# A small store on every DMA engine, and gamma in four pieces, at the start of an RMSNorm + SiLU kernel

**The chip, the cores, the metric.** One core of one Trainium2 chip. The metric is device time of one execution in microseconds (us); less is better. "Span" is what the profile covers, from the first to the last instruction; time was about 1.8 us more than the span (319.27 against 317.5 in the execution profiled before the change).

## The reference

```python
def reference(x, gamma, eps):          # x: 8 x 1024 x 2048 float32, gamma: 2048
    rms = np.sqrt(np.mean(x ** 2, axis=-1, keepdims=True) + eps)
    out = gamma * x / rms
    return (out * (1 / (1 + np.exp(-out)))).astype(np.float32)
```

Each of the 8192 rows is read once and written once: 67.11 MB in and 67.11 MB out.

## The kernel before

The rows are cut into 16 blocks of 4 MB: 128 partitions with 4 rows, 32 KB, each. Six buffers go round. SP issues the loads, ACT the stores. A load into a buffer waits until the store of the block before it in that buffer has landed (store 0 landed at 64.32 us, and load 6 was issued at 64.38). Gamma is put into all 128 partitions (`g`): it is loaded into one partition, spread by matmuls with a column of ones into PSUM, and copied.

```python
    def load(b):
        xt = pool.tile([P, J * d], f32, name="xt")     # P=128, J=4, d=2048; 6 buffers
        nc.sync.dma_start(out=xt, in_=xb[b])
        blocks[b] = xt
    ...
    def store(b):
        nc.scalar.dma_start(out=ob[b], in_=blocks[b])
        if b + LEAD < nblk:                            # LEAD = 6
            load(b + LEAD)
    ...
        grow = pool.tile([P, J * d], f32, name="xt")
        nc.scalar.dma_start(out=grow[0:1, 0:d], in_=<gamma as one row>)
        for b in range(min(LEAD, BUFS - 1)):           # loads 0 to 4
            load(b)
        nc.vector.memset(ones, 1.0)
        for c in range(0, d, 512):
            nc.tensor.matmul(junk_v[:, c:c + 512], ones, grow[0:1, c:c + 512], start=True, stop=True)
        nc.vector.tensor_copy(out=g, in_=junk_v)
        load(BUFS - 1)
        last = nblk - 1
        sums(0)          # sums of squares: row 3 on DVE, rows 0 to 2 on ACT
        ...
```

Of the kernel before, what the change touches and what calls it, by code (L numbers as in the profile page):

```python
# [1 line left out]

# [4 lines left out]

ACT = mybir.ActivationFunctionType
ALU = mybir.AluOpType


@with_exitstack
def kernel(
    ctx: ExitStack,
    tc: tile.TileContext,
    x: bass.AP,
    gamma: bass.AP,
    eps: bass.AP,
    out: bass.AP,
):  # L20





    nc = tc.nc
    P = nc.NUM_PARTITIONS
    f32, i32 = mybir.dt.float32, mybir.dt.int32
    x2 = x.flatten_outer_dims()
    o2 = out.flatten_outer_dims()  # L30
    n, d = x2.shape
    J = 4
    BUFS, LEAD = 6, 6
    nblk = n // (P * J)
    xb = x2.rearrange("(b p j) d -> b p (j d)", p=P, j=J)
    ob = o2.rearrange("(b p j) d -> b p (j d)", p=P, j=J)

    singles = ctx.enter_context(tc.tile_pool(name="singles", bufs=1))
    pool = ctx.enter_context(tc.tile_pool(name="pool", bufs=BUFS))
    small = ctx.enter_context(tc.tile_pool(name="small", bufs=2))  # L40
    psum = ctx.enter_context(tc.tile_pool(name="psum", bufs=1, space=bass.MemoryType.PSUM))

    g = singles.tile([P, d], f32)
    ones = singles.tile([1, P], f32)
    junk_a = psum.tile([P, d], f32, name="junk_a")
    junk_v = psum.tile([P, d], f32, name="junk_v")
    blocks, sss, rstds = {}, {}, {}

    def load(b):
        xt = pool.tile([P, J * d], f32, name="xt")  # L50
        nc.sync.dma_start(out=xt, in_=xb[b])
        blocks[b] = xt

    def row(b, j):
        return blocks[b][:, j * d:(j + 1) * d]

    def rsqrt(ss):


        var = small.tile([P, J], f32, name="var")  # L60
        nc.vector.tensor_scalar(out=var, in0=ss, scalar1=1.0 / d, scalar2=float(eps),  # L61
                                op0=ALU.mult, op1=ALU.add)
        y = small.tile([P, J], f32, name="y")
        t = small.tile([P, J], f32, name="t")
        nc.vector.tensor_single_scalar(out=t.bitcast(i32), in_=var.bitcast(i32), scalar=1,  # L65
                                       op=ALU.logical_shift_right)
        nc.vector.tensor_scalar(out=y.bitcast(i32), in0=t.bitcast(i32), scalar1=-1, scalar2=0x5F375A00,  # L67
                                op0=ALU.mult, op1=ALU.add)
        for _ in range(3):
            nc.vector.scalar_tensor_tensor(out=t, in0=y, scalar=-0.5, in1=y, op0=ALU.mult, op1=ALU.mult)  # L70
            nc.vector.tensor_mul(out=t, in0=t, in1=var)  # L71
            nc.vector.scalar_tensor_tensor(out=y, in0=t, scalar=1.5, in1=y, op0=ALU.add, op1=ALU.mult)  # L72
        return y

    def sums(b, after_first=()):


        ss = small.tile([P, J], f32, name="ss")
        nc.vector.tensor_tensor_reduce(  # L79
            out=junk_v, in0=row(b, J - 1), in1=row(b, J - 1), scale=1.0, scalar=0.0,  # L80
            op0=ALU.mult, op1=ALU.add, accum_out=ss[:, J - 1:J])
        for j in range(J - 1):
            nc.scalar.activation(out=junk_a, in_=row(b, j), func=ACT.Square,  # L83
                                 accum_out=ss[:, j:j + 1])
            if j == 0:
                for s in after_first:
                    store(s)
        sss[b] = ss

    def finish(b, pieces=1):  # L90
        for j in range(J):
            nc.vector.tensor_mul(out=row(b, j), in0=row(b, j), in1=g)  # L92
            nc.scalar.activation(out=row(b, j), in_=row(b, j), func=ACT.Silu,  # L93
                                 scale=rstds[b][:, j:j + 1])
            if pieces > 1 and (j + 1) % (J // pieces) == 0:
                w = J // pieces * d
                i = (j + 1) // (J // pieces) - 1
                nc.scalar.dma_start(out=ob[b][:, i * w:(i + 1) * w], in_=blocks[b][:, i * w:(i + 1) * w])  # L98

    def store(b):  # L100
        nc.scalar.dma_start(out=ob[b], in_=blocks[b])  # L101
        if b + LEAD < nblk:
            load(b + LEAD)

    with tc.manual_schedule():
        grow = pool.tile([P, J * d], f32, name="xt")
        nc.scalar.dma_start(out=grow[0:1, 0:d],
                            in_=bass.AP(tensor=gamma.tensor, offset=gamma.offset, ap=[[d, 1], gamma.ap[0]]))
        for b in range(min(LEAD, BUFS - 1)):
            load(b)  # L110
        nc.vector.memset(ones, 1.0)  # L111
        for c in range(0, d, 512):
            nc.tensor.matmul(junk_v[:, c:c + 512], ones, grow[0:1, c:c + 512], start=True, stop=True)  # L113
        nc.vector.tensor_copy(out=g, in_=junk_v)  # L114
        load(BUFS - 1)


        last = nblk - 1
        sums(0)
        rstds[0] = rsqrt(sss[0])  # L120
        finish(0)
        sums(1)
        rstds[1] = rsqrt(sss[1])
        for b in range(1, last - 1):
            sums(b + 1, after_first=[b - 1])
            finish(b)
            rstds[b + 1] = rsqrt(sss[b + 1])
        store(last - 2)
        finish(last - 1)
        store(last - 1)  # L130
        sums(last)
        rstds[last] = rsqrt(sss[last])
        finish(last, pieces=2)


# [1 line left out]
_INS = ['x', 'gamma', 'eps']  # L137
_OUTS = [((8, 1024, 2048), 'float32')]

_NUMBERS = {'eps': 9.999999747378752e-06}  # L140


# [26 lines left out]
```

## Time and profile before

| | |
|---|---|
| time, 3 runs known at the prediction | 317.92 us median (317.8 to 318.91) |
| time of the execution that was profiled | 319.27 us |
| span of that execution | 317.5 us |
| data through the 16 DMA engines | 134.26 MB, mean 423 GB/s |
| busiest compute engine | ACT, 70% |

The rows of the profile are shown in the prediction below. The DMA row in tenths is full from the second slice to the last but one, and the two data queues hold 98.4% of the engines' span, so the kernel is bound by the DMA engines. The page does not print single packets; the trace has a record of each (queue, start, duration, size), and much of what follows is read from these. A 32 KB packet on an undisturbed engine takes 1.213 us (96% of them in the profile before).

### The profile page before, as it was taken

What the parts mean: (1) busy time and instruction counts of PE and PEld (TensorE: products, weight loads), DVE (VectorE), ACT (ScalarE), POOL (GpSimd) and SP (SyncE); (2) the same over time, 40 slices, a digit from 0 to 9 for tenths busy, and PEclk for the clock granted to TensorE, in tenths of its full rate; (3) what the DMA queues carried; (4) which work ended last, traced back from release to release, by engine and by line L of the source; (5) the groups of instructions that cost most, each with busy time, mean ns of one, the idle gap of its engine ahead of it and who ended that gap; (6) DMA issues with size and microseconds to landing.
All of it is one profiled execution on the core that took longest, in us unless ns stands there. A gap on an engine that the chain in (4) does not pass through costs nothing.

```text
span 317.5 us, 603 instructions
## 1 busy us (share of the span) xinstructions
PE 7.2 (2%) x8; PEld 2.5 (1%) x8; DVE 210.3 (66%) x290; ACT 221.3 (70%) x162; POOL 0.2 (0%) x4
## 2 busy tenths in 40 slices
PE   6200000000000000000000000000000000000000
PEld 2000000000000000000000000000000000000000
DVE  0559299999892947839287392974929559946600
ACT  1359989999892947939388393984929659794800
POOL 0000000000000000000000000000000000000000
DMA  8999999999999999999999999999999999999994
GB/s 327 429 433 433 425 392 455 405 454 417 442 430 433 425 438 425 433 446 425 438 425 439 417 442 433 425 458 417 442 417 446 413 446 433 430 446 425 438 411 204
DMA packets 4758, 134.26 MB, mean 423 GB/s; under 512 B 529, under 2 KB 529, under 8 KB 529
## 3 DMA queue, kind: packets, MB, share of 16 engines
q1 hardware_dynamic: 2304, 67.11, 49.4%
q10 hardware_dynamic: 2450, 67.12, 49.0%
q14 instruction: 4, 0.03, 0.0%
HBM read 67.12 MB, written 67.11 MB: 423 GB/s over the span
## 4 chain that ended last, share of the span: by engine, by line
DMA 73%; DVE 11%; ACT 7%; issue 3%; DVEq 1%; ACTq 0%; SPq 0%
DMA xt<-in_x_dram 39%; DMA out_dram<-xt 34%; DVE xt L92 8%; ACT junk_a L83 5%; ACT xt L93 3%; DVE junk_v L79 1%; DVEq L164 1%; DVE t L70 0%; DVE t L71 0%; DVE y L72 0%; DVE t L65 0%; DVE y L67 0%; DVE var L61 0%; ACTq L98 0%; ACTq L101 0%
## 5 line engine op out<-in xcount | busy, mean ns | idle before, releaser
L92 DVE TENSOR_TENSOR xt<-xt,g 128x2048 f32<-128x2048 f32 x64 | 142.3, 2285 | 0.0
L83 ACT ACTIVATE junk_a<-xt 128x2048 f32<-128x2048 f32 x48 | 90.3, 1881 | 65.5 <-DMA xt<-in_x_dram 64.0
L93 ACT ACTIVATE xt<-xt,y 128x2048 f32<-128x2048 f32 x64 | 124.0, 1992 | 13.0 <-DVE xt L92 13.0
L79 DVE CUSTOM_DVE_ANT_0 junk_v<-xt 128x2048 f32<-128x2048 f32 x16 | 36.8, 2299 | 57.5 <-DMA xt<-in_x_dram 57.5
L61 DVE TENSOR_SCALAR var<-ss 128x4 f32<-128x4 f32 x16 | 2.6, 166 | 15.7 <-ACT junk_a L83 15.7
L83 ACT ACTIVATION_READ_ACCUMULATOR junk_a<-xt 128x1 f32 x48 | 9.0, 187 | 0.0
L72 DVE SCALAR_TENSOR_TENSOR y<-t,y 128x4 f32<-128x4 f32 x48 | 7.8, 162 | 1.7
L70 DVE SCALAR_TENSOR_TENSOR t<-y 128x4 f32<-128x4 f32 x48 | 7.8, 162 | 1.7
L71 DVE TENSOR_TENSOR t<-t,var 128x4 f32<-128x4 f32 x48 | 7.8, 162 | 1.6
L114 DVE COPY g<-junk_v 128x2048 f32<-128x2048 f32 x1 | 2.3, 2292 | 8.7 <-PE junk_v L113 8.7
L113 PE MATMUL junk_v<-xt,ones 1*128 1x512 f32 x8 | 7.2, 1072 | 2.5 <-DMA xt<-in_gamma_dram 2.5
L67 DVE TENSOR_SCALAR y<-t 128x4 int32<-128x4 int32 x16 | 2.7, 170 | 0.5
L65 DVE TENSOR_SCALAR t<-var 128x4 int32<-128x4 int32 x16 | 2.7, 170 | 0.5
L113 PEld LDWEIGHTS junk_v<-xt,ones 1*128 1x128 f32 x8 | 2.5, 325 | 5.6 <-issue 5.6
L79 DVE DVE_READ_ACCUMULATOR2_ANT ss<- 128x1 f32 x16 | 2.3, 142 | 0.0
L83 ACT ACT_TABLE_LOAD x1 | 1.3, 1283 | 1.3 <-PEq L150 1.3
L93 ACT ACT_TABLE_LOAD x1 | 1.3, 1283 | 0.0
L111 DVE MEMSET ones<- 1x128 f32 x1 | 0.2, 165 | 0.8 <-PEq L150 0.8
L150 POOL MEMSET const-bfloat16-1.0<- 128x1 bf16 x1 | 0.1, 102 | 0.0
L150 POOL MEMSET const-uint8-127<- 128x1 uint8 x1 | 0.1, 102 | 0.0
L150 POOL MEMSET const-float32-0.0<- 128x1 f32 x1 | 0.1, 100 | 0.2 <-issue 0.2
L150 POOL MEMSET const-float32-1.0<- 128x1 f32 x1 | 0.1, 99 | 0.0
## 6 DMA issues: line engine op xcount, KB each, us to landing
xt<-in_x_dram SPq DMA_DIRECT2D x16, 4096.0 KB, 36.8
out_dram<-xt ACTq DMA_DIRECT2D x15, 4096.0 KB, 40.6
out_dram<-xt ACTq DMA_DIRECT2D x2, 2048.0 KB, 15.4
xt<-in_gamma_dram ACTq DMA_DIRECT2D x1, 8.0 KB
```

Source lines behind the costliest of these rows:

```text
L61: nc.vector.tensor_scalar(out=var, in0=ss, scalar1=1.0 / d, scalar2=float(eps), op0=ALU.mult, op1=ALU.add)
L65: nc.vector.tensor_single_scalar(out=t.bitcast(i32), in_=var.bitcast(i32), scalar=1, op=ALU.logical_shift_right)
L67: nc.vector.tensor_scalar(out=y.bitcast(i32), in0=t.bitcast(i32), scalar1=-1, scalar2=0x5F375A00, op0=ALU.mult, op1=ALU.add)
L70: nc.vector.scalar_tensor_tensor(out=t, in0=y, scalar=-0.5, in1=y, op0=ALU.mult, op1=ALU.mult)
L71: nc.vector.tensor_mul(out=t, in0=t, in1=var)
L72: nc.vector.scalar_tensor_tensor(out=y, in0=t, scalar=1.5, in1=y, op0=ALU.add, op1=ALU.mult)
L79: nc.vector.tensor_tensor_reduce(out=junk_v, in0=row(b, J - 1), in1=row(b, J - 1), scale=1.0, scalar=0.0, op0=ALU.mult, op1=ALU.add, accum ...
L83: nc.scalar.activation(out=junk_a, in_=row(b, j), func=ACT.Square, accum_out=ss[:, j:j + 1])
L92: nc.vector.tensor_mul(out=row(b, j), in0=row(b, j), in1=g)
L93: nc.scalar.activation(out=row(b, j), in_=row(b, j), func=ACT.Silu, scale=rstds[b][:, j:j + 1])
L113: nc.tensor.matmul(junk_v[:, c:c + 512], ones, grow[0:1, c:c + 512], start=True, stop=True)
L164: with _tile.TileContext(nc) as tc:
```

## The change

Its intent: an early store on each engine should make the first large store cheap, and gamma should no longer stand in front of everything on the ACT queue. The second memset of `seed` only makes DVE wait until the small store has landed (7.36 us in the profile after). Store 0 overwrites what the small store wrote.

```diff
--- before.py
+++ after.py
@@ -41,7 +41,8 @@
     psum = ctx.enter_context(tc.tile_pool(name="psum", bufs=1, space=bass.MemoryType.PSUM))
 
     g = singles.tile([P, d], f32)
-    ones = singles.tile([1, P], f32)
+    ones = singles.tile([P, P], f32)
+    seed = singles.tile([16, P], f32)
     junk_a = psum.tile([P, d], f32, name="junk_a")
     junk_v = psum.tile([P, d], f32, name="junk_v")
     blocks, sss, rstds = {}, {}, {}
@@ -103,14 +104,26 @@
             load(b + LEAD)
 
     with tc.manual_schedule():
+
+
+
+
+        Q = 4
+        w = d // Q
         grow = pool.tile([P, J * d], f32, name="xt")
-        nc.scalar.dma_start(out=grow[0:1, 0:d],
-                            in_=bass.AP(tensor=gamma.tensor, offset=gamma.offset, ap=[[d, 1], gamma.ap[0]]))
-        for b in range(min(LEAD, BUFS - 1)):
+        for b in range(BUFS - 1):
             load(b)
         nc.vector.memset(ones, 1.0)
-        for c in range(0, d, 512):
-            nc.tensor.matmul(junk_v[:, c:c + 512], ones, grow[0:1, c:c + 512], start=True, stop=True)
+        nc.vector.memset(seed, 0.0)
+        nc.scalar.dma_start(out=ob[0][0:16, 0:P], in_=seed)
+        nc.scalar.activation(out=junk_a[:, 0:1], in_=ones[:, 0:1], func=ACT.Square)
+        nc.scalar.dma_start(out=grow[0:P:P // Q, 0:w],
+                            in_=bass.AP(tensor=gamma.tensor, offset=gamma.offset, ap=[[w, Q], [1, w]]))
+        for c in range(Q):
+            k = c * (P // Q)
+            nc.tensor.matmul(junk_v[:, c * w:(c + 1) * w], ones[k:k + 1, :], grow[k:k + 1, 0:w],
+                             start=True, stop=True)
+        nc.vector.memset(seed, 0.0)
         nc.vector.tensor_copy(out=g, in_=junk_v)
         load(BUFS - 1)
 
```

## The prediction

The forecast came to 0.4 x 316.7 + 0.3 x 316.0 + 0.25 x 317.9 + 0.05 x 319.5 = 316.9, shaded to 316.6.

> **What bounds the kernel now.** I read the page from the top: busy times, the 40 slices, the queues, the chain. Then the timeline of the start, the table of windows around the first store and at the end, and last the packet records of the trace.
>
> The page, busy times, slices, queues and chain:
>
> ```profile
> PE 7.2 (2%) x8; PEld 2.5 (1%) x8; DVE 210.3 (66%) x290; ACT 221.3 (70%) x162; POOL 0.2 (0%) x4
> ...
> DMA  8999999999999999999999999999999999999994
> GB/s 327 429 433 433 425 392 455 405 454 417 442 430 433 425 438 425 433 446 425 438 425 439 417 442 433 425 458 417 442 417 446 413 446 433 430 446 425 438 411 204
> ...
> q1 hardware_dynamic: 2304, 67.11, 49.4%
> q10 hardware_dynamic: 2450, 67.12, 49.0%
> ...
> DMA 73%; DVE 11%; ACT 7%; issue 3%; DVEq 1%; ACTq 0%; SPq 0%
> ```
>
> No compute engine is above 70%; the DMA row is full in every slice but the first and the last; 73% of the chain is transfer. The two queues, loads (q1, issued by SP) and stores (q10, issued by ACT), together hold 98.4% of the engines' span. So time can only come from the DMA engines: their start, their stalls, and how evenly the 16 of them end.
>
> The records make that a sum. Nearly every data packet is 32 KB and takes 1.213 us. Each engine carries (67.11 + 67.11) MB / 16 = 8.39 MB, which is 256 such packets: 256 x 1.213 = 310.5 us. The span is 317.5, so all that any change of order can win lies in the other 7.0 us. The records carry no engine number, but a packet starts within some 10 ns of the end of the one before on its engine, so I chained them, and read the 16 completion records of each transfer as the 16 engines' ends. What I found of the 7.0 us:
> - The first data packet starts at about 1.7 us.
> - An engine's first load packet takes 1.5 to 2.1 us in place of 1.213, mostly 0.6 to 0.8 more.
> - Store 0 is issued at 38.48. Just before its first packet, every engine's load packets stretch. Over the last two of them 15 engines lose 0.48 to 0.84 us, mean 0.66. The sixteenth, which came to this point last, has one packet of 2.976 us: 1.76 lost, and its store packets stand one turn further back.
> - At the end the 16 completions of the last store lie from 0.5 before to 2.75 us behind their median: next to last 1.30, last 2.75. The laggard ends at 316.2, the median engine at 313.5. The lag of the last engine on q10 is already 2.60 us when store 0 completes.
> - From the last byte to the end of the span 1.3 us.
>
> The check for a median engine: 1.8 + 310.5 + 0.6 + 0.66 = 313.6, against 313.5 read.
>
> Windows (columns: stretch, its length, busy time of PE, PEld, DVE, ACT, POOL, then clock, DMA share, GB/s):
>
> ```profile
> 38.00:39.00 1.00, 0.00 (x0) 0.00 (x0) 0.46 (x3) 0.97 (x3) 0.00 (x0) 1.00 0.83 360
> 39.00:40.00 1.00, 0.00 (x0) 0.00 (x0) 0.83 (x6) 1.00 (x1) 0.00 (x0) 1.00 0.99 393
> 40.00:41.00 1.00, 0.00 (x0) 0.00 (x0) 0.86 (x6) 0.97 (x3) 0.00 (x0) 1.00 0.88 360
> 41.00:42.00 1.00, 0.00 (x0) 0.00 (x0) 1.00 (x1) 1.00 (x1) 0.00 (x0) 1.00 1.82 524
> 42.00:43.00 1.00, 0.00 (x0) 0.00 (x0) 1.00 (x3) 0.97 (x3) 0.00 (x0) 1.00 0.00 0
> ...
> 312.00:313.00 1.00, 0.00 (x0) 0.00 (x0) 0.00 (x0) 0.00 (x0) 0.00 (x0) 1.00 0.99 426
> 313.00:314.00 1.00, 0.00 (x0) 0.00 (x0) 0.00 (x0) 0.00 (x0) 0.00 (x0) 1.00 0.20 82
> 314.00:315.00 1.00, 0.00 (x0) 0.00 (x0) 0.00 (x0) 0.00 (x0) 0.00 (x0) 1.00 0.08 33
> 315.00:316.00 1.00, 0.00 (x0) 0.00 (x0) 0.00 (x0) 0.00 (x0) 0.00 (x0) 1.00 0.08 33
> ```
>
> A packet's bytes and time stand at its start, so single microseconds are rough; 1.82 and then 0.00 at 41 to 43 means that packets started and no successor did for over a microsecond. At the end the DMA share falls from 0.99 to 0.20 and then 0.08, a little over 1/16: one engine works alone for two microseconds.
>
> [...]
>
> **The change part by part.** The start before, in the timeline:
>
> ```profile
> 0.74 0.52 ACTq L107 DMA_DIRECT2D xt<-in_gamma_dram  x1
> 0.81 0.17 DVE L111 MEMSET ones<- 1x128 f32 x1 [0.81 <-PEq L150]
> 1.30 1.28 ACT L83 ACT_TABLE_LOAD   x1 [1.30 <-PEq L150]
> ...
> 2.53 7.16 PE L113 MATMUL junk_v<-xt,ones 1*128 1x512 f32 x8 [2.53 <-DMA xt<-in_gamma_dram]
> ...
> 9.73 2.29 DVE L114 COPY g<-junk_v 128x2048 f32<-128x2048 f32 x1 [8.75 <-PE junk_v L113]
> 13.18 1.88 ACT L83 ACTIVATE junk_a<-xt 128x2048 f32<-128x2048 f32 x1 [10.60 <-DMA xt<-in_x_dram]
> ```
>
> 1. Gamma moves back. ACT now waits for two memsets of about 0.17 us (until some 1.2), issues the seed store (about 0.5, until 1.7), loads its table (1.28, until 3.0), does a one-column Square (0.2) and issues gamma at about 3.2. Gamma then queues behind load packets: store 0 had its first packet some 4.5 us after its issue, against 0.9 for gamma at the empty start. I estimate gamma landed at 7 to 9 us instead of 2.4, the eight matmuls (7.16) done by 14 to 16, and the copy (2.29) by 16.5 to 18.5 instead of 12.0. Block 0 lands at 13.2, and DVE has 2.3 + 0.14 of summing to do, so until 19 to 21. ACT needs until 19.3 for its three sums anyway. Block 0 is late by 0 to 2 us. If matmuls in four different row groups run beside each other, less.
> 2. That delay is off the path. Store 0, issued at 38.5, would go out by 40.5, with loads 3 to 5 still queued. Load 6 needs store 0 landed, at 64.3; by the completion records load 5 ran until about 81, so there are some 15 us of slack. At the end the last piece is issued at 301.1 and its packets start near 308: several microseconds more. Cost 0.
> 3. Bytes: the seed store adds 16 x 512 B, which is 0.02 us per engine at the measured rate. Four pieces of 2 KB in place of 8 KB on one engine: 0.45 us less on that engine, about 0.1 more on four. That engine is not the laggard. Sum about 0.
> 4. The extra memset of seed makes DVE wait for the seed store, which lands some microseconds after its issue, before the copy of gamma is ready. It, and store 0's wait for the same transfer, cost 0.
> 5. What is meant to pay: the first store of every engine comes at 2 to 4 us, not at 41 to 44. That the stall belongs to the first store, not to a first use of the ACT queue, I infer so: the engine that had carried gamma on q10 was stalled like the rest, since all 16 show at least 0.48. Two effects are to be separated. The mean 0.66 us: it moves to the start, where each engine loses 0.6 to 0.8 on its first load already, so it may be hidden under that, or simply be paid earlier. And the laggard's extra of 1.76 - 0.66 = 1.1 to 1.2 us, about one 32 KB packet[...].
>
> **The rivals.** (a) The stall is paid early by all, but no engine loses a turn of a large packet. The last engine ends 1.2 earlier: 317.9 - 1.2 = 316.7. I favour this[...]. (b) It is hidden under the first load as well: 0.66 more, 316.0.[...] (c) The stall recurs at the first large store[...], or a laggard arises from something else (1.30 us of the second laggard does, and four instruction fetches of 0.31 us fall on some engine): 317.9. (d) Late gamma delays store 0 into something I take for slack: up to 2 us, 319 to 320; the slack of 15 us speaks against it.
>
> **Range and chances.** With weights 0.4, 0.3, 0.25, 0.05 for (a) to (d): 0.4 x 316.7 + 0.3 x 316.0 + 0.25 x 317.9 + 0.05 x 319.5 = 316.9; as the change was plainly aimed at this stall, I shade it to 316.6. A range from 315.2 (hidden, and the second laggard smaller too) to 318.1. Faster by 2% needs 311.6, which is 1.1 above the bare transfer of 310.5 and not to be had with 1.7 at the start and 1.3 at the end: 0.01. Slower by 2%, 324.3, would need the DMA engines idle for 6 us: 0.01.
>
> **What would show it.** In the profile after: gamma issued after the table load, matmuls some 5 us later, copy ending at 16 to 19; store 0 out at 38.5 to 40.5; no stretched load packets around the first large store, and slice 6 at about 430 instead of 392 GB/s; stretched packets at 2 to 6 us instead; a last engine 1.3 to 1.6 us behind the median in place of 2.75. I am wrong if the stretched packets are still there at store 0, if another engine comes in 2.5 us late all the same, or if the share of DMA drops between 12 and 300 us.

The traces show this: gamma before is one 8 KB packet of 0.452 us; in the kernel after, 16 rows are 16 packets of 512 B and four rows four of 2 KB; from 43 us on a chained engine alternates load and store packets; a table load takes 1.28 us. "A turn" is one packet of that alternation. That the laggard lost a turn is the author's estimate, from its 1.1 to 1.2 us beside the 1.213 of a packet; so is that the small store would spare it, from the 0.02 us for 512 B at the measured rate. (a) was favoured because the losses of the other 15 engines, 0.48 to 0.84 us, looked alike. The weight of (b), that the loss is hidden, is an estimate for which nothing measured stands.

## The result

| | median | range | runs |
|---|---|---|---|
| before | 318.55 us | 317.8 to 319.18 | 6 |
| after | 319.31 us | 318.21 to 319.82 | 6 |

The ratio of after to before is 1.0022, with a 95% interval from 0.9999 to 1.0044: the same within 2%, and if anything slower. A ratio here is the mean time of one kernel's fast runs over that of the other's in the same rounds, so it isn't quite the ratio of the medians. The measured time is outside the predicted range, 315.2 to 318.1, and no gain shows.

The page of the kernel after, the same rows as the prediction shows of before:

```profile
PE 2.1 (1%) x8; PEld 0.5 (0%) x8; DVE 210.6 (67%) x292; ACT 221.4 (70%) x163; POOL 0.2 (0%) x4
...
GB/s 329 416 448 415 452 394 440 419 448 419 439 420 439 427 435 427 439 427 448 423 444 440 423 439 423 439 427 435 427 435 427 435 427 445 427 452 427 435 415 261
...
q1 hardware_dynamic: 2304, 67.11, 49.6%
q10 hardware_dynamic: 2488, 67.13, 49.3%
...
DMA 73%; DVE 11%; ACT 7%; issue 3%; DVEq 1%; ACTq 0%; SPq 0%
```

Nothing moved between engines except that PE needs 2.1 us in place of 7.2. The sixth slice still stands at 394 GB/s (392 before), where the prediction wanted about 430. The span of this execution is 316.2 us, so it looks 1.3 us *better* than the profile before (317.5), while the medians say the opposite.

The start, in the timeline of the kernel after (start, duration, engine, line, instruction, and in brackets the wait before it):

```profile
0.95 0.17 DVE L117 MEMSET seed<- 16x128 f32 x1
1.15 0.40 ACTq L118 DMA_DIRECT2D out_dram<-seed  x1
1.58 1.28 ACT L119 ACT_TABLE_LOAD   x1 [1.58 <-DVE seed L117]
1.66 1.07 ACTq L120 DMA_DIRECT2D xt<-in_gamma_dram  x1
...
8.48 0.17 DVE L126 MEMSET seed<- 16x128 f32 x1 [7.36 <-DMA out_dram<-seed]
...
10.61 2.09 PE L124 MATMUL junk_v<-xt,ones 1*128 1x512 f32 x8 [10.61 <-DMA xt<-in_gamma_dram]
12.76 2.29 DVE L127 COPY g<-junk_v 128x2048 f32<-128x2048 f32 x1 [4.12 <-PE junk_v L124]
```

Gamma lands 8 us later than before (10.61 us against 2.53), but the matmuls, which now read partitions 0, 32, 64 and 96 (the prediction's four row groups) and not partition 0 alone, run beside each other: eight matmuls take 2.09 us together, with 1133 ns for one of them, against 7.16 us together before, with 1072 ns for one. The copy ends at 15.05, and store 0 goes out at 38.57, against 38.48 before.

The windows around store 0 and at the end, for the kernel after (columns as in the prediction):

```profile
41.00:42.00 1.00, 0.00 (x0) 0.00 (x0) 1.00 (x1) 1.00 (x1) 0.00 (x0) 1.00 1.73 524
42.00:43.00 1.00, 0.00 (x0) 0.00 (x0) 1.00 (x1) 0.97 (x3) 0.00 (x0) 1.00 0.00 0
...
313.00:314.00 1.00, 0.00 (x0) 0.00 (x0) 0.00 (x0) 0.00 (x0) 0.00 (x0) 1.00 0.20 82
314.00:315.00 1.00, 0.00 (x0) 0.00 (x0) 0.00 (x0) 0.00 (x0) 0.00 (x0) 1.00 0.08 33
315.00:316.00 1.00, 0.00 (x0) 0.00 (x0) 0.00 (x0) 0.00 (x0) 0.00 (x0) 1.00 0.00 0
```

From 42 to 43 no packet starts on any engine, exactly as before: the stretched load packets in front of store 0 are still there. At the end the lone last engine stops one microsecond earlier. In packet records, chained by engine (L load, S store, start in us + duration in ns), a typical engine of before, the engine of before with the longest packet (the laggard), and a typical engine of after and the one that came to store 0 last:

```
before, typical   L38.75+1213 L39.96+1456 L41.42+1786 S43.20+1213 L44.41+1213 S45.62+1213
before, laggard   L39.25+1213 L40.46+1213 L41.68+2976 L44.65+1213 S45.86+1213 L47.07+1213
after, typical    L38.76+1213 L39.97+1273 L41.25+1793 S43.04+1213 L44.25+1213 S45.46+1213
after, last       L39.51+1213 L40.72+1213 L41.94+1986 S43.92+1213 L45.13+1213 S46.34+1213
```

In this execution of the kernel after no engine had a packet near 3 us. Was that the change, or luck?

### The profile page after: what moved, and what is told of

Read it like the earlier page. It is cut to its first block, busy times and chain, and to the rows that moved or that the text cites. A ratio compares the mean times of both kernels' runs of the same rounds, so it can differ in the third digit from the quotient of the medians.

```text
span 316.2 us, 609 instructions
## 1 busy us (share of the span) xinstructions
PE 2.1 (1%) x8; PEld 0.5 (0%) x8; DVE 210.6 (67%) x292; ACT 221.4 (70%) x163; POOL 0.2 (0%) x4
## 4 chain that ended last, share of the span: by engine, by line
DMA 73%; DVE 11%; ACT 7%; issue 3%; DVEq 1%; ACTq 0%; SPq 0%
DMA xt<-in_x_dram 41%; DMA out_dram<-xt 32%; DVE xt L93 8%; ACT junk_a L84 5%; ACT xt L94 3%; DVE junk_v L80 1%; DVEq L177 1%; DVE t L71 0%; DVE t L72 0%; DVE y L73 0%; DVE t L66 0%; DVE y L68 0%; DVE var L62 0%; ACTq L102 0%; ACTq L99 0%
## 5 line engine op out<-in xcount | busy, mean ns | idle before, releaser
L124 PE MATMUL junk_v<-xt,ones 1*128 1x512 f32 x8 | 2.1, 1133 | 10.6 <-DMA xt<-in_gamma_dram 10.6
L124 PEld LDWEIGHTS junk_v<-xt,ones 1*128 1x128 f32 x8 | 0.5, 306 | 10.6 <-issue 10.6
```

The costliest lines, as they stand in the source:

```text
L124: nc.tensor.matmul(junk_v[:, c * w:(c + 1) * w], ones[k:k + 1, :], grow[k:k + 1, 0:w], start=True, stop=True)
```

## The experiments

Sixteen runs were made, in four calls on four chips; each call was compared with its own runs of the kernel before. "Stretch" is the time that load packets took over 1.213 us between 38 and 50 us, as a mean over the 16 engines. Theory 1: no part of the change reaches the end, and which engine lags is a matter of the execution. Theory 2: the change has a cost of its own. Third is the prediction's theory, that the early store removes the stretch and with it the laggard.

### First call: the null test, and the change in halves

**before_again**: no edit.

> The kernel before, unchanged, as the null test and for a second set of packet records. Both theories: ratio 1.000, inside about 0.998 to 1.002. If the laggard engine of the first profile (2.75 us behind the median at the end) belongs to the kernel, the new records show it again, 2.5 us or more; if it is a matter of one execution (that profiled execution took 319.27 us, the median 317.92), the last engine may now be 1 to 2 us behind.

Measured: ratio 0.9999 (0.9987 to 1.0011); median 318.0 us against 317.99. Its profile has no packet above 1.94 us before store 0, and its last engine ends 1.33 us behind the median instead of 2.75. So the laggard that the prediction was built on is not in every execution of that same kernel.

**after_again**: the changed kernel, no edit.

> The changed kernel, unchanged. Theory 1 (no part of the change reaches the end; which engine lags is a matter of the execution): ratio 1.000, between 0.998 and 1.002. Theory 2 (the change has a small cost of its own at the start): 1.002 again, 1.001 to 1.004. Theory of the prediction (the early store removes a lagging engine): 0.994 to 0.997. In the records all expect the load packets to stretch by about 0.65 us before store 0, as in the first profile after, except the prediction's theory.

Measured: 1.0022 (1.0008 to 1.0037). The stretch is 0.95 us per engine. The prediction's theory is refuted: the stretch is there and the time isn't less.

**seed_only**: the small store alone.

```diff
+    seed = singles.tile([16, P], f32)
         nc.vector.memset(ones, 1.0)
+        nc.vector.memset(seed, 0.0)
+        nc.scalar.dma_start(out=ob[0][0:16, 0:P], in_=seed)
...
+        nc.vector.memset(seed, 0.0)
         nc.vector.tensor_copy(out=g, in_=junk_v)
```

> The kernel before with the 512-byte store per engine alone added; gamma stays first and in one row. Theory 1: 1.000. Theory 2, if the store is what costs: 1.001 to 1.004; if late gamma costs: 1.000. Prediction's theory: 0.994 to 0.997. In the records I expect the stretch before store 0 to be there as in the others, 0.5 to 0.8 us per engine.

Measured: 1.0019 (1.0007 to 1.0031), stretch 0.82 us.

**gamma_only**: the changed kernel without `seed`, its memsets and its store.

> Gamma in four pieces behind the table load, without the small store. Theory 1: 1.000. Theory 2, if late gamma costs: 1.001 to 1.004; if the store costs: 1.000. Gamma should land at about 10 us, the matmuls take some 2 us, and store 0 should go out at 38.5 as before.

Measured: 1.001 (0.9995 to 1.0026), stretch 0.58 us. Gamma's four 2 KB packets ran at 6.1 to 6.2 us and the matmuls began at 7.99, earlier than the 10 us expected; store 0 went out at 38.25. The later gamma is hidden, as predicted.

What follows: on this chip the small store with its two memsets brought a slowdown of about 0.6 us, and gamma nothing that can be told from zero. The records showed one thing more, on the queue that the page calls q14 "instruction"; its 8 KB packets are called fetches here. In the kernel before there are four in the span, 0.31 us each, and the load packet behind each of the first three took 1.46 to 1.76 us in place of 1.213. The kernels with the small store had a fifth 8 KB packet on this queue, 1.7 us after the end of the span, and their time was longer than their span by 2.0 us, not 1.8. The 8 KB instruction packets from the start of the span on, from the trace records, with two kernels of later calls:

```
                 starts of the packets, us            span, us
before_again     49.3  85.7  166.3  275.0              316.1
after            49.3  88.5  166.3  263.4   317.9      316.2
two_memsets      49.2  88.0  166.6  276.1   319.7      317.9
after_pool       49.5  88.2  166.5  263.1              317.2
```

### Second call: what of it is the store, and what could prepare an engine

**two_memsets**: `seed_only` without the store.

> The kernel before with the change's two extra memsets on DVE and nothing else: no store. The kernels with the small store showed a fifth 8 KB instruction fetch, 1.7 us after the last instruction of the span, and time minus span of about 2.0 us against 1.8. [...]this kernel shows the fifth fetch too, time minus span is 2.0, span 316.2 as before, and the ratio is about 1.0006. If the fetch belongs to the store, there are four fetches and 1.8.

The cut is a guess at the mechanism, which no run shows; what follows it is the case in which the fetch comes with the two DVE instructions.

Measured: the fifth fetch is there (at 319.7 us, span 317.9). Time minus span is 1.94 us on average over 6 runs, against 1.79 for the 11 runs of before. So this 0.15 to 0.2 us comes with the two DVE instructions and not with the store. It isn't in every run: the six run from 1.75 to 2.17 us, those of before from 1.73 to 1.82. The ratio, 1.000 (0.9978 to 1.0021), is too wide to show it. The profiled execution also had a laggard: one load packet of 3.002 us before store 0, last engine 2.99 us behind, 319.79 us.

**seed_pool**: `seed_only` with both memsets on POOL.

> The small store with its two memsets on POOL, so that DVE has no instruction more. If the store itself costs: span about 316.7 against 316.2, time minus span 1.8, ratio about 1.0013 to 1.002. If the whole cost came with the DVE instructions: ratio 1.000 (0.999 to 1.001). The stretch of the load packets before store 0 should be there, 0.55 to 0.95 us per engine.

Measured: 1.0007 (0.9989 to 1.0025), time minus span 1.78, four fetches, stretch 0.74. And a laggard, *with* the small store: a packet of 2.867 us, last engine 2.47 us behind. The interval doesn't decide between the two expectations.

**full_packet_seed**: in place of 512 B, 32 KB on each engine, when block 0 has landed.

```diff
         last = nblk - 1
+        nc.scalar.dma_start(out=ob[0][0:16, :], in_=blocks[0][0:16, :])
         sums(0)
```

> The kernel before with a store of 16 raw rows of block 0, 32 KB on each engine, when load 0 has landed (13 us); store 0 overwrites them. Theory A (a stretch belongs to the first packet of full size that joins a running load stream, each time the store queue was empty): load packets stretch by 0.5 to 0.9 us per engine at about 14 to 18 us, and again before store 0 at 40 to 44 us. Theory B (only the first large store of an execution pays): stretch at 14 to 18, none at 40 to 44. Theory C (the stretch belongs to the 4 MB transfer[...]): none at 14 to 18, 0.5 to 0.9 at 40 to 44. Time: one packet more per engine, 1.2 us, so ratio about 1.004 under C, 1.006 under A, 1.004 under B.

In theory C a guess at what in the transfer would do it is cut.

Measured: every load packet from 38 to 50 us takes 1.213 us. The stretch is 0.00, on all 16 engines: theory B, of the three. But its other half did not come as expected: the loads from 13 to 21 us stretched by only 0.04 us per engine, and the early packet itself took 2.6 to 4.1 us, so the kernel loses: 1.009 (1.0069 to 1.011), and not 1.004. The store queue was empty between the two stores (the early packets started before 19 us, store 0 was not issued before 38), so it isn't a matter of the queue being empty (A), nor of the 4 MB transfer (C). Two stretches of 8 us in the windows, for `before_again` and then `full_packet_seed` (last column GB/s):

```profile
13.00:21.00 8.00, 0.00 (x0) 0.00 (x0) 3.97 (x12) 7.26 (x7) 0.00 (x0) 1.00 1.04 451
38.00:46.00 8.00, 0.00 (x0) 0.00 (x0) 7.36 (x16) 7.18 (x9) 0.00 (x0) 1.00 1.00 393
```

```profile
13.00:21.00 8.00, 0.00 (x0) 0.00 (x0) 2.57 (x4) 7.29 (x7) 0.00 (x0) 1.00 1.01 307
38.00:46.00 8.00, 0.00 (x0) 0.00 (x0) 5.68 (x15) 7.91 (x8) 0.00 (x0) 1.00 0.98 422
```

The hole has moved from the second row to the first, and grown. The small store leaves the second row as it was; `seed_only`:

```profile
13.00:21.00 8.00, 0.00 (x0) 0.00 (x0) 3.82 (x11) 7.29 (x7) 0.00 (x0) 1.00 1.03 446
38.00:46.00 8.00, 0.00 (x0) 0.00 (x0) 7.18 (x16) 7.18 (x9) 0.00 (x0) 1.00 1.00 389
```

**two_newton**: two steps in place of three in the reciprocal root (`for _ in range(2)`), 48 DVE instructions fewer.

> The kernel before with two steps in place of three in the reciprocal root: 48 DVE instructions fewer, meant as a test of the instruction fetches (each holds up one engine by 0.3 us and lengthens the packet beside it). DVE should need one fetch fewer in the run (three or fewer in place of four). If fetches make the last engine late: the last engine ends 0.3 to 0.8 us earlier, ratio 0.998 to 0.999. If not: 1.000. Result still correct within the comparison.

Measured: 0.9993 (0.9972 to 1.0014), correct. My expectation of one fetch fewer, an estimate, missed: there are four, but two of them moved, from 49 and 166 us to 59 and 207. Only DVE has fewer instructions, so those two are DVE's; the ones at 88 and 276 stayed and so are most likely another engine's. A gain can't be told from zero.

### Third call: size, time and address of the early store

**small_at_13**: as `full_packet_seed`, but `[0:16, 0:P]`, 512 B per engine. **kb8_at_13**: `[0:16, 0:d]`, 8 KB per engine.

> As the full-size early store (16 rows of block 0, issued when load 0 has landed), but 512 B of each row: place in time, rows and queue are the same, only the size differs. If size decides: load packets before store 0 stretch by 0.55 to 0.95 us per engine again, as after the change's small store. If it was the later time or the source in block 0 that helped: no stretch, 0.00 to 0.05.

> The same with 8 KB of each row. If any store above some kilobytes opens the way: stretch before store 0 is 0.00 to 0.1 us per engine, no packet over 1.5 us there, and the ratio is about 0.998 to 1.001 (0.3 us of packet and a one-time cost of some 0.6 us paid early, no lost turn of a 32 KB packet). If 32 KB are needed: stretch 0.55 to 0.95 and ratio 1.001 to 1.003.

Measured: stretch 0.68 and 0.70 us per engine. Size decides, and 8 KB per engine are not enough; in `kb8_at_13` one engine even had a packet of 2.840 us. Both also became 5 us slower (`small_at_13` 322.91 us in one run, of unknown state; `kb8_at_13` 1.0162, 1.014 to 1.0185), which nobody expected. From 62 us on their load packets stretched again, at about every load of a block, some 4 us per engine in all. Why is open: `full_packet_seed`, of the same build but for the size, doesn't do it.

**other_block_at_13**: as `full_packet_seed`, but into the rows of block 8 (`out=ob[8][0:16, :]`).

> The full-size early store, 32 KB per engine, but into the rows of block 8. If what helps is tied to the addresses written (rows of block 0): stretch of 0.55 to 0.95 us per engine before store 0 is back. If it is a matter of the first large store of an engine, wherever it goes: 0.00 to 0.05, as with block 0's rows. The early packets should take 3 to 4 us again, being read from 16 neighbouring partitions.

Measured: stretch 0.00, early packets 3.1 to 4.1 us, 321.49 us in one run, of unknown state. That the early store goes into another block doesn't matter.

**dram_copy_first**: a copy from x to out inside DRAM, 8 KB per engine, as ACT's first DMA.

```diff
         grow = pool.tile([P, J * d], f32, name="xt")
+        nc.scalar.dma_start(out=ob[0][0:16, 0:d], in_=xb[0][0:16, 0:d])
```

> First on the ACT queue, ahead of gamma: a copy from x to out inside DRAM, 8 KB per engine, with no memset and no SBUF read. If the one-time cost belongs to the write to DRAM: the load packets before store 0 do not stretch (0.00 to 0.1), and as the copy runs beside the first loads' own latency the ratio may be 0.997 to 1.000. If it belongs to the read of SBUF by a large store, or to the size of packets: stretch 0.55 to 0.95 again, ratio 1.001 to 1.003.

Measured: stretch 0.83 us, 1.0008 (0.9984 to 1.0032). Store 0 went out only at 42.44, against 38.48, which cost nothing that can be seen. As 8 KB from SBUF didn't help either, this says nothing on reads against writes.

### Fourth call, with the cause still open

**spread_full_at_13**: as `full_packet_seed`, from every eighth row (`[0:P:8, :]`).

> The full-size early store, 32 KB per engine, from every eighth row of block 0[...]. No stretch before store 0 (0.00 to 0.05 us per engine) as with 16 neighbouring rows. The early packet takes 1.2 to 2.5 us in place of 3.0 to 4.1. If the one-time cost is only moved, early packet and load packets beside it together lose 0.5 to 0.9 us over a plain packet, and the ratio is about 1.004 (1.2 us for the packet). If it is hidden there: 1.002.

Measured: now the early store packets take 1.213 us each, and the load packets in front of them stretch: 0.92 us per engine, between 13 and 21 us, up to 2.26 us for one packet. Before store 0 there is 0.17 left. Ratio 1.0042 (1.0018 to 1.0067). So the cost is moved and not removed, and the packet of 1.2 us comes on top. The windows of `spread_full_at_13`:

```profile
13.00:21.00 8.00, 0.00 (x0) 0.00 (x0) 2.36 (x2) 7.29 (x7) 0.00 (x0) 1.00 1.01 385
38.00:46.00 8.00, 0.00 (x0) 0.00 (x0) 5.41 (x15) 7.87 (x9) 0.00 (x0) 1.00 1.00 422
```

So an early 32 KB packet took 2.6 to 4.1 us from 16 neighbouring rows (`full_packet_seed`) and 1.213 us from every eighth row (here). Why neighbouring rows were slow is not shown, and how much of the slow packets was the one-time cost is not known.

**rows128_1k_at_13**: all 128 rows, 1 KB of each (`[:, 0:256]`), eight packets of 1 KB per engine.

> An early store of all 128 rows, 1 KB of each: eight packets of 1 KB on each engine. If the number of rows[...] opens the way: no stretch before store 0. If the packet size does: stretch of 0.55 to 0.95 us per engine before store 0, as after 512 B and 8 KB. The kernels with 512 B and 8 KB at this place also showed later stretches, one at about each load, and 4 us more in all; I expect them here as well if the stretch before store 0 is there.

Measured: stretch 0.56 us, at the end of that interval, for store 0 went out at 44.60 and its first packets came at about 49 us. Ratio 0.9997 (0.997 to 1.0025). Eight small packets don't prepare an engine. As they are 8 KB per engine in all, this doesn't tell packet size from bytes per engine: 32 KB per engine in smaller packets was not tried. The later stretches that I expected did not come.

**seed_pool_again** and **after_pool**, the latter being the changed kernel with its two memsets on POOL.

> The small store with its memsets on POOL, once more. If the store costs of itself: ratio 1.001 to 1.002, time minus span 1.8. If not: 0.999 to 1.001.

> The changed kernel with the two memsets of seed on POOL in place of DVE. Four instruction fetches, none after the span; time minus span 1.8 in place of 2.0. If the fetch is the part of the cost that is certain: ratio 1.000 to 1.0015, below the 1.0022 of the changed kernel.

Measured: 1.0005 (0.9983 to 1.0027) and 1.0002 (0.998 to 1.0024). Time minus span is 1.80 in both, and `after_pool` has no fetch after the span. The part of time minus span that came with the DVE instructions is gone. Both profiled executions had a laggard (2.984 and 2.954 us).

### All undisturbed profiles together

Thirteen profiled executions have store 0 as their first full-size store, and no later stretches. Sorted by their longest load packet from 38 to 50 us:

| longest packet | kernels (time of that execution, us) | last engine behind the median |
|---|---|---|
| 2.87 to 3.00 us | before (319.27), two_memsets (319.79), seed_pool (319.11), seed_pool_again (319.01), after_pool (319.01) | 2.1 to 3.0 us |
| 1.83 to 2.30 us | before_again (317.91), gamma_only (317.82), after (318.21), after_again (318.55), seed_only (318.84), two_newton (317.91), dram_copy_first (318.56), rows128_1k_at_13 (317.98) | 1.0 to 2.1 us |

Every execution with a packet near 3 us took 319.0 us or more, and every one without took less than 318.9. Three of the five had the small store. The kernel before alone was on both sides. All three with the memsets on POOL lie in the first row, and none of the three with the small store and DVE memsets; these are three executions each, and the runs of the POOL kernels spread from 318.1 to 319.5 us, so whether this is more than chance is open.

## Why the prediction was wrong

- **What bounds the kernel: right.** The records of the kernel after add up as the prediction's sum does. Its median engine ends at 313.54 us; the prediction read 313.5 for before. (One small reading is off: one engine's first load packet took 1.41 us, below the 1.5 to 2.1 given.)
- **Part 1 and 2, gamma: right that it costs nothing.** Gamma landed later than estimated, at 10.6 and not 7 to 9. The matmuls then took 2.09 us and not 7.16, the "less" that the prediction left open, so the copy ended at 15.05, before the estimated 16.5 to 18.5. Store 0 moved by 0.1 us. The slack that rival (d) doubted is real: in `rows128_1k_at_13` store 0 went out at 44.60, 6 us late, and the ratio was 0.9997.
- **Part 3, bytes: right.** The 512-byte packets took 0.027 us each and stretched nothing beside them.
- **Part 4, the extra memset: wrong in a place nobody looked at.** DVE's wait cost nothing, as said. But two more DVE instructions brought a fifth instruction fetch behind the last one, and 0.15 to 0.2 us between span and time. `two_memsets` shows it, and `after_pool` takes it away. That the fetch is what takes the time is argued from their coming together.
- **Part 5, the step that failed first: "the first store of every engine comes at 2 to 4 us, not at 41 to 44", and with it the stall.** The small store did come (at 6 us), but the stretch stayed: 0.62 us per engine after, 0.77 before, and 0.56 to 0.95 over all thirteen executions, with the small store or without. It isn't the first store that pays. It is the first *full-size* store packet that joins running loads: after one of 32 KB the stretch is 0.00 to 0.17, after 512 B, 8 KB or eight times 1 KB it stays at 0.56 to 0.95. (Packet size and bytes per engine were not told apart, and no full-size store was tried without loads beside it. What in the engine causes the loss is not known from these runs.) Rival (c), which the prediction gave a quarter, said that the stall recurs at the first large store; that is what happened. What the runs show is that the loss is not tied to the addresses written, since a store into block 8 helped as much (0.00 us left in `other_block_at_13`), nor to the 4 MB transfer, since one 32 KB packet per engine was enough (0.00 in `full_packet_seed`).
- **The second step that failed: "The last engine ends 1.2 earlier: 317.9 - 1.2 = 316.7".** The pattern was real: with a packet of 2.87 to 3.00 us before store 0 the last engine ended 2.1 to 3.0 us behind the median, in five executions, and without one 1.0 to 2.1 us, in eight. But the laggard was taken from the profile of an execution of 319.27 us and its removal subtracted from the median of others, 317.92. Those were mostly executions without it. That is read from the times, two of the three at 317.8 and 317.92; their packets were not recorded. Both numbers were known at the prediction, and the difference between them, 1.35 us, is about the laggard (2.75 us behind the median in one profile of before, 1.33 in the other). So even a change that removed it for good could not have brought the median of 317.92 down by 1.2.
- **Why after came out slower.** Of the 0.0022, about 0.0006 (0.2 us of 318) is the longer time after the span that comes with the two DVE memsets; that much is shown. For the rest there are two intervals above 1 on one chip, 1.0008 to 1.0037 for `after_again` and 1.0007 to 1.0031 for `seed_only`. Kernels with the store but without the DVE instructions measured 1.0002, 1.0005 and 1.0007 on two others, with 1 inside each interval. Whether the small store costs 0.1 to 0.5 us of its own stays open, and so does the rival that the changed kernel merely met the laggard in more of its executions, since runs without a profile don't show their packets. None of these runs shows a gain.

No experiment led to a kernel that beats both. What was paid once, in each of the thirteen profiles above, is 0.56 to 0.95 us per engine; an early full-size store only moved it (0.92 us at 13 to 21 us in `spread_full_at_13`), and no way to hide it was found.

## What to carry to other kernels

A profile is one execution: before subtracting a lateness that it shows, compare the time of that very execution with the median, and take a second profile of the same kernel. Before warming something up, test with a large and a small dose which of them works, and what the dose itself costs. When microseconds count, count instructions too: two memsets of 0.17 us, off the critical path, came with 0.15 to 0.2 us more of run time after the last visible instruction (`two_memsets`, 1.94 us of time minus span against 1.79).
